# A relative-position bias for attention: one mirrored row in DRAM, read as 128 overlapping rows

## The chip, the cores and the metric

The kernel runs on one core of a Trainium2 chip, in one launch. The metric is the time of one execution on the device in microseconds (us), as a median over runs. Five engines work side by side, each through its own instructions in order: TensorE (PE in the profile; its weight loads are PEld), VectorE (DVE), ScalarE (ACT), GpSimd (POOL) and SyncE (SP), which here only issues transfers. A transfer (DMA) that SyncE issues is carried out by 16 DMA engines; the issuing queue itself goes on, unless the next entry has to wait for something.

## The reference, cut to what matters

The network is two transformer blocks over 512 tokens of width 1024, all in float32. The first block adds three branches: a gated spatial mixer, a pooling branch and a differential attention with 4 heads of two 64-wide score maps each. The attention adds a bias that depends only on the distance between query and key, looked up in 32 buckets per head:

```python
def block(args):
    qi, i = args
    qpos = i * Q_BLOCK + jnp.arange(Q_BLOCK)          # Q_BLOCK = 128
    rel = qpos[:, None] - kpos[None, :]
    bias = rel_bias[t5_causal_bucket(rel)].astype(jnp.float32)
    s = jnp.einsum('bqhcd,bkhcd->bhcqk', qi, k).astype(jnp.float32) * scale
    s = s + bias.transpose(2, 0, 1)[None, :, None]
    s = jnp.where((rel >= 0)[None, None, None], s, -1e30)
    p = jax.nn.softmax(s, axis=-1)
    a = p[:, :, 0] - lam * p[:, :, 1]
    return jnp.einsum('bhqk,bkhd->bqhd', a.astype(v.dtype), v)
```

Since the bias depends on `qpos - kpos` alone, one row of values per head, shifted by one place for each query, holds all of it. Behind the attention come gates, a projection, a gated convolutional feed-forward layer, and a second block with a dilated-window attention and another feed-forward layer, which the change does not touch.

## The kernel before

**Units.** The work is a list of weight units. One unit is one [128, 1024] float32 tile of weights: SyncE loads it (`load`, L165) into one of four buffers `wr`, ScalarE rounds it to its leading part `wh` (L171), VectorE computes the remainder `wl` (L103, called from L178), and TensorE multiplies it in 24 matmuls (three products: leading by leading, leading by remainder, remainder by leading), which take about 5.5 us. The loop at the end of `build` (L1316 to L1336) writes the order out by hand: at each step the matmuls of unit `u`, the rounding of unit `u + 3`, the remainder of `u + 2`, the loads up to unit `u + 6`, then what is done with finished products (`post`), then the fillers that the schedule hangs on that unit (`at(unit, function)`, L1176 to L1242). Every engine and queue works in the order in which this loop emits.

**The order around the change.** The units are `uv0` to `uv3`, `v0` to `v3`, then `q0 k0 q1 k1 b0 b1 q2 k2 q3 k3`, then the gates. `bias_prep` hangs on `v2`. The post of each key unit, `double` (L415 to L425), has ScalarE write a leading part `dbh` (L419) and VectorE a remainder `dbl` (L421), and has SyncE copy each half of both to the other 64 partitions (L424). The first scores, `da_scores(0, 0)`, hang on `k1`; block i of head h comes at unit `k1 + 4h + i`.

**The bias.** `bias_load` fetches a one-hot table `oh` of 33 by 640 and the bucket values `rb`. `bias_prep` multiplies them on TensorE (L504, L505), so that each of four partitions gets the 640 bias values of one head, ordered by position, the last 128 being a large constant that masks the future. VectorE negates them into `bs` (L508, L509). SyncE then writes the four rows to a DRAM tile `bd`, each of them 128 times, one behind the other with a pitch of 641 (L511), and reads each head's area back with a pitch of 640 (L515): row p of the tile `strip[h]` starts one value earlier in the bias row than row p - 1. In `da_scores` the reduction on VectorE (L548) adds a window of the strip to the scores in PSUM and takes the row minimum. It does so twice for each of 4 blocks of 4 heads, 32 times in all, with widths of 128, 256, 384 and 512. ScalarE then takes the exponential, and later units transpose the result and multiply it by the values.

Of the kernel before, what the change touches and what calls it, by code (L numbers as in the profile page):

```python
# [23 lines left out]
F32 = mybir.dt.float32  # L24
# [7 lines left out]
S = 512  # L32
# [23 lines left out]
def build(tc, a):  # L56
    nc = tc.nc
    te, ve, ac, po = nc.tensor, nc.vector, nc.scalar, nc.gpsimd
    ctx = ExitStack()
    with ctx:  # L60
# [58 lines left out]
        def split2(src, name, n=S):  # L119
            """As split; the remainder comes one step later."""  # L120
            hi = slot(name + "h", F32R)
            lo = slot(name + "l", F32R)
            ac.activation(hi[:, :n], src, AF.Copy)
            later(1, tt, lo[:, :n], src, f(hi)[:, :n], OP.subtract)
            return hi, lo

# [1 line left out]
        prm = cp.tile([128, NPRM], F32, name="prm")  # L128
# [14 lines left out]

# [1 line left out]
        units = []  # L145
# [76 lines left out]

# [1 line left out]
        def compact(hl, out, bank=misc):  # L224
            """Sums over the partitions of a [128, 512] tile: [128, 4], token = 128 * column + partition."""
            hi, lo = hl
            p = bank("cs")
            mm(p, onesr, hi, True, False)
            mm(p, onesr, lo, False, True)
            for b in range(4):  # L230
                t = tiny("dg", 128)
                ve.tensor_tensor_reduce(out=t, in0=p[:, 128 * b:128 * b + 128], in1=identf, scale=1.0,
                                        scalar=0.0, op0=OP.mult, op1=OP.add, accum_out=out[:, b:b + 1])
# [4 lines left out]
        def bcast_rows(cols, name):  # L238
            """cols: [128, 4] per-token values -> [128, 512] with them along the free axis."""
            p = misc(name + "p")  # L240
            for b in range(4):
                te.transpose(p[:, 128 * b:128 * b + 128], cols[:, b:b + 1].to_broadcast([128, 128]),
                             identf)
            return p
# [5 lines left out]

        # state shared by the stages
        X, XH, XL = {}, {}, {}
# [17 lines left out]
        def norm_in(m, src, g, key):  # L270
            """hi/lo of src * g, and the square of src."""
            XH[m] = slot("xh", F32R)
            XL[m] = slot("xl", F32R)
            ac.activation(XH[m], src, AF.Copy, scale=g)
            stt(XL[m], src, g, f(XH[m]), OP.mult, OP.subtract)
# [15 lines left out]

        # =================================================================
        # Block 1
        # =================================================================
        UV, GM = {}, {}
# [85 lines left out]

# [1 line left out]
        VH = {}  # L383
# [15 lines left out]
        def stack(src, gain):  # L399
            """Two heads of 64 features: per head the leading part above the remainder (swapped for  # L400
            the second), so that one product over 128 rows takes both."""
            t = duo("stk")
            for e, r, o in halves():
                if gain is None:
                    ac.activation(t[r, e, :], src[r], AF.Copy)
                else:
                    ac.activation(t[r, e, :], src[r], AF.Copy, scale=gain[r])
            for e, r, o in halves():
                if gain is None:
                    tt(t[o, e, :], src[r], f(t)[r, e, :], OP.subtract)  # L410
                else:
                    stt(t[o, e, :], src[r], gain[r], f(t)[r, e, :], OP.mult, OP.subtract)
            return t

        def double(src):  # L415
            """Two heads of 64 features: per head the leading part, and the remainder, in both halves."""
            h, l = duo("dbh"), duo("dbl")
            for e, r, o in halves():
                ac.activation(h[r, e, :], src[r], AF.Copy)  # L419
            for e, r, o in halves():  # L420
                tt(l[r, e, :], src[r], f(h)[r, e, :], OP.subtract)  # L421
            for t in (h, l):
                for e, r, o in halves():
                    nc.sync.dma_start(f(t)[o, e, :], f(t)[r, e, :])  # L424
            return h, l  # L425
# [10 lines left out]

# [1 line left out]
        ZB, YB, pw = {}, {}, {}  # L438
# [49 lines left out]

# [1 line left out]
        strip = {}  # L490
# [10 lines left out]
        def bias_prep():  # L501
# [7 lines left out]
            ve.tensor_scalar(bs[:4, 512:640], p1[:4, :128], -1.0, None, op0=OP.mult)  # L509
            d = dr.tile([4, 128 * 641], F32, name="bd")  # L510
            nc.sync.dma_start(d.rearrange("h (p u) -> h p u", u=641)[:, :, :640],  # L511
                                bs[:4, None, :640].to_broadcast([4, 128, 640]))
            for h in range(4):
                strip[h] = slot("strip")
                nc.sync.dma_start(strip[h], d[h, :128 * 640].rearrange("(p u) -> p u", u=640)[:, 127:639])  # L515

# [15 lines left out]
        def da_scores(h, i):  # L532
# [11 lines left out]
            for c, p in enumerate(pp):  # L544
                if c == 0 or i > 1:
                    ts_ = slot("st")
                t = ts_[:, 256 * c:] if i < 2 else ts_
                ve.tensor_tensor_reduce(out=t[:, :W], in0=p[:, :W], in1=strip[h][:, 384 - 128 * i:],  # L548
                                        scale=1.0, scalar=BIG, op0=OP.add, op1=OP.min,
                                        accum_out=nm[:, c:c + 1])  # L550
                ts.append(t)
# [63 lines left out]

# [1 line left out]
        G, MG = {}, {}  # L617
# [24 lines left out]

# [1 line left out]
        def xhl():  # L644
# [69 lines left out]

# [1 line left out]
        GL, AH, AL = {}, {}, {}  # L716
# [68 lines left out]

        # =================================================================
        # Block 2
        # =================================================================
        st2 = cp.tile([128, 40], F32, name="st2")
# [5 lines left out]
        def b2_stat():  # L795
            """rsqrt of the final norm and of block 2's norm; their product in both token orders."""
            rf, ma, mb, r2 = st2[:, 8:12], st2[:, 12:16], st2[:, 16:20], st2[:, 20:24]
# [42 lines left out]
        def qk_norm(key, scale):  # L840
            """Token-major q/k features [128, 8 x 64] per block -> rms-normalised."""
            def post(p):
# [32 lines left out]
        def qk_tr(key, part, dst, dkey, gain):  # L875
            """Transpose 128 features (2 heads) of all blocks; gain per feature; hi/lo."""
            qs = QK[key]
# [29 lines left out]

        # natural-order part: group 0; statistics per (block, head)
        nst = cp.tile([128, 4, 2, 8], F32, name="nst")
# [26 lines left out]
        def n_tr(pr, j):  # L936
            """Key block j: the queries of blocks j and j+1, per head: [k, (e, q)]."""
            p = misc("ntr")
# [31 lines left out]
        def n_stats(pp):  # L970
            """Statistics of heads 4*pp..4*pp+3 to C order."""
            h = slice(4 * pp, 4 * pp + 4)
# [9 lines left out]
        def c_scores(pr, b0, nb):  # L982
            """Joint softmax of groups 1 and 2 with group 0's statistics, for blocks b = t % 4."""
            w = tp.tile([128, 5, 8], F32, name="cw", tag="cw", bufs=4)
# [61 lines left out]
        def c_tr(pr, b):  # L1046
            """[k, (g, e, q)]"""
            p = misc("ctr")
# [9 lines left out]
        def c_f(pr):  # L1058
            """Group 0's part times its share of the joint softmax."""
            fp = misc("fbp")  # L1060
# [110 lines left out]

        # =================================================================
        # Fillers
        # =================================================================
        L = label
# [67 lines left out]

        # =================================================================
        # Emission
        names.update({v: k for k, v in label.items()})
        # =================================================================
        warm = misc("warm")
# [106 lines left out]
def _layout(inp):  # L1355
# [80 lines left out]
    oh[32, 512:] = 1.0  # L1436
    A["oh"] = oh
    return A
# [16 lines left out]
```

## Time and profile before

| | |
|---|---|
| time, median of 3 runs | 1414.61 us (1413.69 to 1415.21) |
| span of the profiled execution | 1413.5 us; the page gives no other time of it |
| TensorE busy | 1366.0 us, 97% of the span |
| VectorE, ScalarE, GpSimd busy | 57%, 43%, 18% |
| mean granted clock of TensorE | 0.987 |
| the 32 bias reductions (L548) | 284 to 692 ns each, from 116.8 to 217.1 us |
| the write of `bd` (L511) | 1280 KB, issued at 49.6 us |
| the four reads of the strips (L515) | 256 KB each, issued from 102.6 to 103.9 us |

Times in the trace count from the start of the span. A busy matmul's end is modelled, since matmuls are pipelined, so rows of matmuls overlap a little. A row of waits names the waiting operation, its line, and what released it. In the chain of work that ended last, each piece begins where the piece that released it ends.

### The profile page before, as it was taken

To read this page: it belongs to the slowest core of one execution; us is meant where nothing else is said; L and a number is where in the kernel's file an instruction comes from. 1 tells how busy PE (TensorE), PEld (TensorE's weight loads), DVE (VectorE), ACT (ScalarE), POOL (GpSimd) and SP (SyncE) were. 2 spreads that over 40 slices of the span, in tenths; PEclk is the share of its full clock that TensorE was granted. 3 is DMA by queue.
4 is the path that set the end of the run, shared out by engine and by line. 5 is a ranking of instruction groups with operands and counts; after the bars stand their busy time and mean duration, and the time that the engine had idled before them with its cause. 6 is when DMAs were issued, how large, how long until landed. Compare 5 with 4: busy or idle time off the path is not lost.

```text
span 1413.5 us, 16670 instructions
## 1 busy us (share of the span) xinstructions
PE 1366.0 (97%) x6360; PEld 1138.0 (81%) x6360; DVE 808.8 (57%) x1328; ACT 603.3 (43%) x974; POOL 248.9 (18%) x208
## 2 busy tenths in 40 slices
PE   9927999999999999999999999999999999999998
PEld 7816888888888888888888888888878888888887
DVE  6705766555656554553335847567887666665222
ACT  6404654423434333333224657655754444443110
POOL 3204111110111111110113611223061111110000
PEclk9968999999999999999999999999999999999999
DMA  7225422233233323232332333222223333333330
GB/s 251 55 43 159 120 75 89 75 129 125 89 95 100 104 90 105 90 97 82 112 97 75 120 91 90 61 77 73 75 66 99 99 95 98 96 98 93 113 113 32
DMA packets 46692, 135.92 MB, mean 96 GB/s; under 512 B 9923, under 2 KB 10638, under 8 KB 46612
## 3 DMA queue, kind: packets, MB, share of 16 engines
q1 hardware_dynamic: 45556, 132.60, 31.0%
q0 software_dynamic: 912, 2.19, 0.5%
q8 instruction: 50, 0.82, 0.2%
q14 instruction: 30, 0.25, 0.1%
q10 hardware_dynamic: 144, 0.07, 0.0%
HBM read 127.19 MB, written 3.44 MB: 92 GB/s over the span
## 4 chain that ended last, share of the span: by engine, by line
PE 92%; another core or an unknown queue 4%; DVE 2%; DMA 2%; SPq 1%; issue 0%; ACT 0%; DVEq 0%
PE acc L89 84%; PE cs L89 1%; DMA wr<-in_w_uv 1%; PE cu L89 1%; PE qkt L880 1%; PE sc L89 1%; PE nu L89 1%; DVE xl L106 1%; DMA dbl<-dbl 1%; PE ns L89 1%; PE pv L89 1%; PE ctr L1051 0%; PE ms L89 0%; PE ntr L944 0%
## 5 line engine op out<-in xcount | busy, mean ns | idle before, releaser
L89 PE MATMUL acc<-xh,wh 128*128 128x512 f32 x968 | 378.8, 391 | 0.0
L89 PE MATMUL acc<-xl,wh 128*128 128x512 f32 x968 | 377.4, 390 | 0.0
L89 PE MATMUL acc<-xh,wl 128*128 128x512 f32 x968 | 377.3, 390 | 0.0
L103 DVE TENSOR_TENSOR wl<-wr,wh 128x1024 fp32r<-128x1024 f32 (+2 forms) x233 | 297.4, 1277 | 128.6 <-PE acc L89 77.3
L171 ACT ACTIVATE wh<-wr 128x1024 fp32r<-128x1024 f32 (+1 forms) x233 | 242.0, 1039 | 256.6 <-PE acc L89 170.8
L89 PEld LDWEIGHTS acc<-xh,wl 128*128 128x128 f32 x968 | 182.1, 188 | 38.2
L89 PEld LDWEIGHTS acc<-xh,wh 128*128 128x128 f32 x968 | 182.2, 188 | 37.4
L89 PEld LDWEIGHTS acc<-xl,wh 128*128 128x128 f32 x968 | 182.2, 188 | 37.3
L89 PE MATMUL acc<-al,wh 128*128 128x512 f32 (+1 forms) x358 | 138.0, 385 | 0.0
L89 PE MATMUL acc<-ah,wl 128*128 128x512 f32 (+1 forms) x358 | 138.0, 385 | 0.0
L89 PE MATMUL acc<-ah,wh 128*128 128x512 f32 (+1 forms) x358 | 138.0, 385 | 0.0
L720 ACT ACTIVATE cv<-z,prm 128x512 f32<-128x512 f32 x66 | 53.7, 816 | 165.7 <-DVE z L103 165.7
L106 DVE SCALAR_TENSOR_TENSOR cv<-z,prm,cv 128x511 f32<-128x511 f32 (+1 forms) x132 | 99.6, 756 | 2.4
L89 PEld LDWEIGHTS acc<-ah,wh 128*128 128x128 f32 x358 | 67.2, 188 | 13.6
L89 PEld LDWEIGHTS acc<-al,wh 128*128 128x128 f32 x358 | 67.2, 188 | 13.5
L89 PEld LDWEIGHTS acc<-ah,wl 128*128 128x128 f32 x358 | 67.2, 188 | 13.4
L89 PE MATMUL acc<-wh,ch 128*128 128x512 f32 x192 | 75.8, 395 | 0.0
L89 PE MATMUL acc<-wl,ch 128*128 128x512 f32 x192 | 74.9, 390 | 0.0
L89 PE MATMUL acc<-wh,cl 128*128 128x512 f32 x192 | 74.8, 390 | 0.0
L103 POOL TENSOR_TENSOR gl<-cv,r2b 128x512 f32<-128x512 f32 x22 | 28.4, 1291 | 202.9 <-ACT cv L734 202.9
L103 POOL TENSOR_TENSOR act<-cv,cv 128x512 f32<-128x512 f32 x22 | 28.4, 1292 | 202.0 <-DVE cv L106 188.4
L236 POOL TENSOR_TENSOR rr<-ss,mh 128x8 f32<-128x8 f32 x24 | 38.8, 1645 | 114.1 <-DVE ss L852 114.1
(333 smaller groups left out, 1958.1 us busy)
## 6 DMA issues: line engine op xcount, KB each, us to landing
wr<-in_w_up SPq DMA_DIRECT2D x88, 512.0 KB, 3.5
wr<-in_w_dn SPq DMA_DIRECT2D x32, 512.0 KB, 3.5
wr<-in_w_g SPq DMA_DIRECT2D x24, 512.0 KB, 3.5
wr<-in_w_qkc SPq DMA_DIRECT2D x16, 512.0 KB, 3.5
wr<-in_w_o SPq DMA_DIRECT2D x12, 512.0 KB, 3.6
wr<-in_w_dn SPq DMA_DIRECT2D x16, 384.0 KB, 3.1
wr<-in_w_qkn SPq DMA_DIRECT2D x8, 512.0 KB, 4.2
wr<-in_w_vc SPq DMA_DIRECT2D x8, 512.0 KB, 3.4
```

Of the source, the lines that this page charges most:

```text
L89: te.matmul(out, l, r, start=start, stop=stop, skip_group_check=True)
L103: (eng or ve).tensor_tensor(out, x, y, op=op)
L106: ve.scalar_tensor_tensor(out, x, s, y, op0=o0, op1=o1)
L171: ac.activation(hi[:, :n], raws[j][:, :n], AF.Copy)
L236: po.tensor_tensor(out, src, mh[:, :n], op=OP.pow)
L720: ac.activation(c, z, AF.Identity, scale=P(cw, 2 * n + j), bias=P(cb, j))
L880: te.transpose(p[:, 128 * b:128 * b + 128], qs[b][:, 128 * part:128 * part + 128], identf)
```

## The change

The bias row of each head is written to DRAM once, as one row of 640, and the one-hot table is built in reverse order on the host, so the row is mirrored. The strip's row p is read from position p + 1 of that row, 512 values on: 128 overlapping rows with a step of one value. The mirrored strip therefore has to be read from right to left, which a hand-made access pattern with a step of -1 (`mirrored`) does in the bias reduction. Block i uses the first 128 (i + 1) values of the strip, where it used the last ones before. The diff also takes out comments and docstrings, which are not shown.

```diff
@@ bias_prep
-            d = dr.tile([4, 128 * 641], F32, name="bd")
-            nc.sync.dma_start(d.rearrange("h (p u) -> h p u", u=641)[:, :, :640],
-                                bs[:4, None, :640].to_broadcast([4, 128, 640]))
+            d = dr.tile([4, 640], F32, name="bd")
+            nc.sync.dma_start(d, bs[:4, :640])
             for h in range(4):
                 strip[h] = slot("strip")
-                nc.sync.dma_start(strip[h], d[h, :128 * 640].rearrange("(p u) -> p u", u=640)[:, 127:639])
+                row = d[h:h + 1, :]
+                nc.sync.dma_start(strip[h], bass.AP(row.tensor, row.offset + 1, [[1, 128], [1, S]]))
+
+        def mirrored(t, n):
+
+            x = t[:, n - 1:n]
+            return bass.AP(x.tensor, x.offset, [list(x.ap[0]), [-1, n]])
@@ da_scores
-                ve.tensor_tensor_reduce(out=t[:, :W], in0=p[:, :W], in1=strip[h][:, 384 - 128 * i:],
+                ve.tensor_tensor_reduce(out=t[:, :W], in0=p[:, :W], in1=mirrored(strip[h], W),
                                         scale=1.0, scalar=BIG, op0=OP.add, op1=OP.min,
                                         accum_out=nm[:, c:c + 1])
@@ _layout
-    A["oh"] = oh
+    A["oh"] = np.ascontiguousarray(oh[:, ::-1])
```

## The prediction

> **What bounds the kernel now.** I read the page's busy shares first, then the waits of the matmul engine, the chain of work that ended last around the largest of them, the stretches on both sides of it, and the SyncE queue that the chain runs through.
>
> The page: TensorE works 97% of the span, so only a hole in its work, or a lower clock, can be won back. The figures of the DMA issues are KB and median us from issue to landing.
>
> ```profile
> span 1413.5 us, 16670 instructions
> PE 1366.0 (97%) x6360; PEld 1138.0 (81%) x6360; DVE 808.8 (57%) x1328; ACT 603.3 (43%) x974; POOL 248.9 (18%) x208
> dbh<-dbh SPq DMA_DIRECT2D x16, 128.0 KB, 2.3
> bd<-bs SPq DMA_DIRECT2D x1, 1280.0 KB
> wr<-in_w_b SPq DMA_DIRECT2D x2, 512.0 KB, 4.5
> strip<-bd SPq DMA_DIRECT2D x4, 256.0 KB, 3.4
> out_dram<-out SPq DMA_DIRECT2D x7, 256.0 KB, 2.0
> lnrow<-in_lnrow POOLq DMA_DIRECT2D x1, 256.0 KB, 10.4
> ws<-in_wsT POOLq DMA_DIRECT2D x1, 256.0 KB, 11.2
> dst__90<-nst SPq DMA_DIRECT2D x4, 8.0 KB, 3.7
> d<-st SPq DMA_DIRECT2D x1, 2.0 KB, 8.8
> ```
>
> The waits (total us, times, longest). TensorE's largest is one wait of 35.9 us for the duplicated key tile `dbh`; ScalarE lost 42.2 us to a weight load, and SyncE's queue 52.1 us to the write of `bd`.
>
> ```profile
> PE sc L89 <- DMA dbh<-dbh: 35.9, 1, 35.9
> PE sc L89 <- DMA dbl<-dbl: 0.8, 1, 0.8
> ACT wh L171 <- DMA wr<-in_w_b: 42.2, 1, 42.2
> SPq L515 <- DMA bd<-bs: 52.1, 1, 52.1
> ```
>
> The chain (start, length, what) shows these as one event. The 52.14 us piece has no record of its own: it is the write issued at 49.61 under way. Behind it in the queue stand the strip reads, weight loads, and only then the `dbh` and `dbl` copies (L424) that the first scores need.
>
> ```profile
> 49.61 0.82 SPq L511
> 50.44 52.14 another core or an unknown queue
> 102.97 0.43 SPq L515
> ...
> 105.83 0.66 SPq L424
> 106.58 0.54 SPq L424
> 107.21 8.61 DMA dbl<-dbl
> 115.86 0.93 PE sc L89 x3
> 116.80 7.06 PE acc L89 x24
> 123.86 0.47 PE sc L89 x4
> ...
> 142.33 0.40 PE sc L89 x4
> 142.73 5.50 PE acc L89 x24
> 148.23 0.47 PE sc L89 x4
> ```
>
> The stretches (length, then busy us and count of PE, PEld, DVE, ACT, POOL, granted clock, DMA share, GB/s): full before, empty for 35.9 us, then 9.1 us at a mean clock of 0.70, then full again.
>
> ```profile
> 47.60:78.70 31.10, 31.07 (x145) 25.07 (x144) 17.83 (x41) 9.95 (x19) 0.25 (x1) 1.00 0.25 40
> 78.70:114.60 35.90, 0.02 (x1) 0.06 (x1) 3.20 (x4) 3.26 (x4) 0.00 (x0) 0.55 0.45 108
> 114.60:123.70 9.10, 8.26 (x29) 6.72 (x30) 4.22 (x9) 4.17 (x9) 0.00 (x0) 0.70 0.70 218
> 123.70:220.00 96.30, 96.30 (x460) 80.70 (x459) 70.62 (x169) 55.32 (x118) 23.84 (x25) 1.00 0.29 88
> ```
>
> The write moves 1280 KB in 52.14 us, 25 GB/s, in 4 x 128 rows of 2560 B, with the DMA engines 25% busy in the stretch that holds its start. A quarter of 16 is four engines, so 128 rows each and 52.14 / 128 = 0.407 us a row.
>
> **The change part by part.** *The write.* 512 rows become 4, and 1280 KB become 10 KB. It is still issued once, after the same two VectorE copies. At the rate just found, one row for each of four engines costs 0.4 us beside the landing. The trace shows no 10 KB write of this shape; the bounds are 2.0 us (`out`, 256 KB) and 8.8 us (`d<-st`, 2 KB in single words). I take the nearest row in size and direction, 3.7 us (`dst__90<-nst`, 8 KB): landing at 49.61 + 3.7 = 53.3, with 51.6 and 58.4 as ends.
>
> *The reads.* Still four of 256 KB and 128 rows of 2048 B, with a row step of 4 B instead of 2560 B, all out of 2560 B of DRAM. The rows that decide whether this crawls:
>
> ```profile
> 102.59 1.76 SPq L515 DMA_DIRECT2D strip<-bd  x4
> 104.46 0.37 SPq L165 DMA_DIRECT2D wr<-in_w_b  x1
> 66.22 1.28 ACT L419 ACTIVATE dbh<-kt 64x512 fp32r<-64x512 f32 x2 [3.07 <-DVE kt L103]
> 77.64 1.03 PE L376 MATMUL gtr<-identf,gy 128*128 128x128 f32 x8
> L548 DVE CUSTOM_DVE_ANT_0 st<-sc,strip 128x512 f32<-128x512 f32 x8 | 5.2, 688 | 0.2
> L548 DVE CUSTOM_DVE_ANT_0 st<-sc,strip 128x128 f32<-128x128 f32 x8 | 2.0, 288 | 2.1 <-PE sc L89 2.1
> L103 DVE TENSOR_TENSOR gz<-acc,r1b 128x512 f32<-128x512 f32 x8 | 5.5, 690 | 12.3 <-PE acc L89 12.3
> ```
>
> `lnrow` reads one 2 KB row 128 times and landed in 10.4 us, no slower than `ws`, with 128 different rows, in 11.2 us in the same crowded start. So I take 3.4 us, the price of the old strip reads. Ends: 2.0 us (nothing lands sooner here), and one read at 25 GB/s, 10.4 us.
>
> *What stood behind them on SyncE.* The four issues take 1.76 us: 53.3 to 55.1 (60.2 at worst), all landed by about 59. The load of `w_b` follows 0.1 us later, takes 0.37 us to issue and 4.5 us to land: about 60.1, at worst 65.2. Its first reader, ScalarE, is at the key cast of row L419 until 66.22 + 1.28 = 67.5 anyway. So 42.2 us of ScalarE's wait go with 7.4 us in hand (2.3 at worst). Two more weight loads follow; they wait only for their buffers, as in every unit. The `dbh` copies can then go when the cast is done, 67.5, and land 2.3 us later, near 70. `dbl` stands two issues behind (0.66 + 0.54), at 68.7; even at the 8.61 us that it took in the crowd of the chain above it lands by 77.3. TensorE comes to the first scores at 77.64 + 1.03 = 78.7, so 1.4 us are in hand at the worst. VectorE wants the first strip about 81, after the next key's remainders, 22 us after landing.
>
> *TensorE.* From 78.68 it runs what it now runs from 78.68 + 35.9 = 114.58 to 123.86: the four score matmuls of block 0 and one weight unit. The same pair undisturbed stands at 142.33: 0.40 + 5.50 = 5.90 us. So this piece ends at 84.58 instead of 123.86: **39.28 us less**. Of these, 35.9 + 0.8 are the waits; the other 2.5 are matmuls at the low clock after the hole (the unit took 7.06 instead of 5.50; the scores, from 114.58 to 116.80, took 2.22 with the 0.84 of wait, instead of 0.40). These go too, because the clock was 1.00 in the stretches on both sides of the hole.
>
> *The mirrored operand.* 32 score reductions read the strip with step -1. Forward, the widths 512 and 128 take 688 and 288 ns: 400 ns for 384 columns, 1.04 ns each, over 8 x (128 + 256 + 384 + 512) = 10,240 columns 10.7 us in all. No instruction of this trace reads backwards. The lower end is no change: a gain is excluded, since a different two-input operation of 512 columns takes the same 690 ns (`gz`), so the columns, not the order, set the price. The upper end is open; at twice the price it is 10.7 us of VectorE. I take no change, since addresses a word apart are just as near in either direction. Cover: from 123.7 to 220 VectorE is busy 70.62 of 96.3 us, so 25.7 us are free and the twofold price is hidden. Without that cover the cost would be the whole 10.7 us.
>
> [...]
>
> *The rest* (the one-hot table built backwards on the host, comments taken out, a smaller DRAM tile) adds no instruction: nothing.
>
> *Sum.* 1413.5 - 39.3 = 1374.2 us of span. The page gives no time of the profiled execution beside its span; the runs' median, 1414.61, stands 1.1 above it, so I forecast 1414.61 - 39.28 = **1375.3 us**. Late next would be nothing in this place: what follows it in the trace of before, from 123.7 to 220, has TensorE busy for 96.30 of 96.30 us, and its feeders work in step with it. Own range 1373.3 to 1378: 2 below for the spread of the runs (1413.69 to 1415.21), 2.7 above for a short wait that the hole covered.
>
> **The rivals.**
>
> *Something else is late near 79 (part of the gain).* The engines behind TensorE would go without the pause. For it: ScalarE and VectorE queues are in order, and the transposes' evacuation and the first reductions fall together. Against: they stood still in the hole too (3.3 and 3.2 us of work in 35.9), so they gained no lead from it. Price: a wait of 3 to 10 us, and with a long one a low clock after it as now (2.5): 1378 to 1388.
>
> *The overlapping reads crawl.* The write was slow; if the cause was that 512 packets went through one small place and not that four engines did the work, the reads will do the same. For: 25 GB/s. Against: `lnrow`. The price at 25 GB/s: 4 x 256 KB = 1.05 MB in 41.7 us, from 53.4 to 95.1; then the copies land 2.3 to 8.6 us later, 97.4 to 103.7, instead of at 115.86: a gain of 12 to 18, **1396 to 1403**.
>
> [...]
>
> *The write is not what is slow (the change doesn't do what it says).* If the 52 us were a fixed delay of a DRAM write by SyncE before its readers may go, the four rows would wait as long. Against: the `dst` write and its like land in 3.7 us, and the DMA bytes flow evenly at 25 GB/s. The time would be 1414.6.
>
> *Slower: the mirrored read makes VectorE the bound.* With r times the price a column, VectorE gets (r - 1) x 10.7 us more and has 25.7 us to spare: it decides from r = 3.4, and undoes the gain at (r - 1) x 10.7 = 25.7 + 39.3, r = 7.1. At r = 8 the time is 1375.3 + 74.9 - 25.7 = **1424**. For it: nothing in the trace reads backwards. Against: a step back of one word would have to cost seven steps forward, and no row here hints at a price for the order.
>
> **How the numbers follow.** The forecast 0.85; a smaller late wait 0.06; the crawl 0.05; no effect 0.01; slower 0.03. The range must leave out no more than 0.2. The forecast with its own range leaves out 0.15 and what falls beyond its ends; I take 1373.3 to 1380, which reaches into the small-wait case and leaves out the crawl and the slow mirror. A change within 0.2% is 2.8 us, about what this measurement can tell from none. Faster: 0.85 + 0.06 + 0.05 = 0.96. Same 0.01. Slower 0.03.
>
> **What the changed profile would show.** The wait of SyncE's queue at the strip reads falls from 52.1 us to 2 to 9 us; the strip issues stand near 53, not 102.59; the 35.9 us wait for `dbh` is gone from TensorE's list and the chain has no unknown piece; the granted clock stays 1.00 through 47 to 220 us; the strip reads land in about 3.4 us; the L548 groups keep 688 and 288 ns. The prediction is wrong if the strips land over 10 us, if the first scores wait for a copy, or if L548 takes more than three times as long.

## The result, and the profile after

| | before | changed |
|---|---|---|
| time, median | 1414.28 us (1413.69 to 1415.21, 4 runs) | 1375.25 us (1374.88 to 1375.68, 4 runs) |
| ratio | | 0.9721, 95% interval 0.9707 to 0.9735 |
| span of the profiled execution | 1413.5 us | 1373.8 us |

The forecast was 1375.3 us. The page and the transfer list of the changed kernel: the span is 39.7 us shorter at nearly the same TensorE work (1363.8 against 1366.0 us), so a hole was closed.

```profile
span 1373.8 us, 16670 instructions
PE 1363.8 (99%) x6360; PEld 1137.4 (83%) x6360; DVE 808.5 (59%) x1328; ACT 603.2 (44%) x974; POOL 248.7 (18%) x208
strip<-bd SPq DMA_DIRECT2D x4, 256.0 KB, 4.0
bd<-bs SPq DMA_DIRECT2D x1, 10.0 KB
```

What SyncE's queue waited for between 47 and 80 us, and what it issued. The wait for the write fell from 52.1 to 1.1 us. The strip reads follow the write by 1.50 us from issue to issue, not 52.98, and the key copies go as soon as their data are cast, at 66.39.

```profile
SPq L165 <- DVE wl L103: 17.2, 4, 6.5
SPq L424 <- ACT dbh L419: 4.5, 2, 2.4
...
SPq L515 <- DMA bd<-bs: 1.1, 1, 1.1
```

```profile
49.12 0.33 SPq L511 DMA_DIRECT2D bd<-bs  x1
50.62 1.77 SPq L515 DMA_DIRECT2D strip<-bd  x4
52.49 0.38 SPq L165 DMA_DIRECT2D wr<-in_w_b  x1
...
66.39 1.18 SPq L424 DMA_DIRECT2D dbh<-dbh  x2
67.66 1.19 SPq L424 DMA_DIRECT2D dbl<-dbl  x2
```

The chain at the same place and the stretches: the transposes (`gtr`), the first scores and the unit behind them stand end to end, 0.40 + 5.51 us, and the clock is 1.00 from 47 to 220 us.

```profile
77.31 0.87 PE gtr L376 x8
78.18 0.40 PE sc L89 x4
78.58 5.51 PE acc L89 x24
84.09 0.47 PE sc L89 x4
```

```profile
78.70:84.60 5.90, 5.90 (x29) 4.98 (x28) 4.70 (x10) 4.20 (x10) 0.00 (x0) 1.00 0.71 191
47.00:220.00 173.00, 173.00 (x824) 144.14 (x823) 121.25 (x274) 90.62 (x179) 33.76 (x32) 1.00 0.34 101
```

The unit behind the first scores ends at 84.09 instead of 123.86: 39.77 us, of which 0.49 is an earlier arrival (the bias product started at 47.23 instead of 47.72). The difference, 39.28, is the prediction's sum. That it agrees to the last digit is partly luck: between the medians the gain is 39.03 us, and between the spans 39.7. The backward reductions, now L553, cost what the forward ones did:

```profile
L553 DVE CUSTOM_DVE_ANT_0 st<-sc,strip 128x512 f32<-128x512 f32 x8 | 5.2, 687 | 0.2
...
L553 DVE CUSTOM_DVE_ANT_0 st<-sc,strip 128x128 f32<-128x128 f32 x8 | 2.0, 287 | 2.0 <-PE sc L89 1.9
```

### The profile page after: what moved, and what is told of

It reads as the page before. It is cut to its first block, busy times and chain, and to the rows that moved or that the text cites. A ratio compares the mean times of both kernels' runs of the same rounds, so it can differ in the third digit from the quotient of the medians.

```text
span 1373.8 us, 16670 instructions
## 1 busy us (share of the span) xinstructions
PE 1363.8 (99%) x6360; PEld 1137.4 (83%) x6360; DVE 808.5 (59%) x1328; ACT 603.2 (44%) x974; POOL 248.7 (18%) x208
## 4 chain that ended last, share of the span: by engine, by line
PE 98%; DVE 1%; issue 0%; ACT 0%; DMA 0%; DVEq 0%; POOLq 0%
PE acc L89 89%; PE ms L89 2%; PE cs L89 1%; PE cu L89 1%; PE qkt L885 1%; PE nu L89 1%; PE sc L89 1%; PE ns L89 1%; PE pv L89 1%; DVE xl L106 1%; PE ctr L1056 0%; PE ntr L949 0%; PE tr L583 0%; DVE y L103 0%; DMA g<-in_prm 0%
```

## The experiments

The theory: the write of 512 rows by four DMA engines held SyncE's queue, and all that stood behind it came late; overlapping reads and the backward operand (the strip read from right to left) cost nothing. Rivals: the reads or the backward operand have prices of their own; many packets from one small place are slow whatever the engines; the bias data themselves were late, not the queue.

**How much of the write hurts: 128, 64 and 32 copies.** The changed kernel with the write blown up again; only the first copy is read.

```diff
-            d = dr.tile([4, 640], F32, name="bd")
-            nc.sync.dma_start(d, bs[:4, :640])
+            d = dr.tile([4, 128, 640], F32, name="bd")      # or 64, or 32
+            nc.sync.dma_start(d, bs[:4, None, :640].to_broadcast([4, 128, 640]))
...
-                row = d[h:h + 1, :]
+                row = d[h, 0:1, :]
```

> The changed kernel, but the four rows are written 128 times again (unused beyond the first); mirrored row, overlapping reads and backward reduction stay. If the write alone made the hole, the strip reads are issued 53 us after the write again and the time is that of before, 1414.3 us within 1.5. If the overlapping reads or the backward operand gave or cost anything of their own, it lies off 1414.3 by that amount.

> The changed kernel with 64 copies. From the two traces the strip reads follow the write by 52.98 us for 128 copies and 1.50 for one, 0.405 us a copy; 64 copies give 27.0 us, strip reads at 76.1. Before, the first scores could run 12.0 to 13.3 us after the first strip read was issued: 88 to 89.4 here, against 78.2 undisturbed. So a hole of about 11 us and some 2 us of low clock: 1388 us (1385 to 1391). If every microsecond of the write cost one, it would be 1375.3 + 25.5 = 1400.8.

> The changed kernel with 32 copies: strip reads at 63.2, everything behind them landed by 76.4, before TensorE needs it at 78.2. If the slack of the prediction is real, 12.6 us more of write cost nothing: 1375.3 us within 1.5. If every microsecond of the write cost one: 1387.8.

Measured, against 1415.11 us of the kernel before on the same chip: 128 copies 1417.7 us (ratio 1.0017, 1.0007 to 1.0027), 64 copies 1393.09 (0.9844, 0.9829 to 0.9859), 32 copies 1378.17 (0.9736, 0.9722 to 0.9751). From the write's issue to the strip reads it took 52.98, 27.38 and 14.57 us, so 0.400 us for each copy from 32 on. The rows for 64 copies:

```profile
49.15 0.83 SPq L511 DMA_DIRECT2D bd<-bs  x1
76.53 1.76 SPq L515 DMA_DIRECT2D strip<-bd  x4
78.39 0.37 SPq L165 DMA_DIRECT2D wr<-in_w_b  x1
81.58 1.54 SPq L424 DMA_DIRECT2D dbh<-dbh  x2
83.22 1.34 SPq L424 DMA_DIRECT2D dbl<-dbl  x2
```

The shape is the theory's, a slack and then a slope: 32 copies cost about 3 us, the next 32 cost 15, the next 64 cost 25, which is 0.38 us a copy. But each time lies above what was expected, by 3 to 5 us; 0.8 us of this is the level of the series, whose kernel before took 1415.11 and not 1414.28. The transfer rows show one more cause: in these three kernels the strips landed in 5.9, 5.6 and 5.4 us, against 3.4 before, and the transfers behind them were held up. The rows above have the key copies issued 5.05 us after the strip reads (76.53 to 81.58); in the kernel before it was 3.24 us. The 32-copy kernel's list of TensorE's waits has `dbl` at 0.9 us, where the expectation had it land in time. Its bias product also started at 49.04, 1.8 us later than in the changed kernel's trace; the start of the program moves by that much between traces. Of the 3.2 us by which its span is longer (1377.0 against 1373.8), 1.8 thus stand ahead of the write and 0.9 are the wait, so 3 us probably overstates what 32 copies cost.

**What makes the reads slow.** 128 copies, mirrored row and backward reduction as above, but row p of a strip comes from copy p.

```diff
-                nc.sync.dma_start(strip[h], bass.AP(row.tensor, row.offset + 1, [[1, 128], [1, S]]))
+                nc.sync.dma_start(strip[h], bass.AP(row.tensor, row.offset + 1, [[641, 128], [1, S]]))
```

> The kernel with 128 copies and the mirrored row again, but row p of a strip is read from copy p (row step 641 values) instead of all from the first copy; the backward reduction stays. With all rows from one copy the strips landed in 5.9 us at 143 to 225 GB/s, against 3.4 us at 330 to 430 GB/s in the kernel before, and the time was 0.17% above that of before. If many rows from one place are what is slow, the strips land in about 3.4 us again, the wait for dbh is about 36 us and not 39, and the time is that of before. If the backward operand cost those 2.6 us, the time stays 0.17% above and the landing at about 3.4 or 5.9 either way.

Measured: 1414.47 us against 1415.42 before, 0.9994 (0.9985 to 1.0004). TensorE's long wait was 37.1 us, between the 36 that was expected and the 39.0 of overlapping rows. The strips land as before the change; first this kernel's row, then that of the kernel with 128 copies whose rows overlap:

```profile
strip<-bd SPq DMA_DIRECT2D x4, 256.0 KB, 3.5
```

```profile
strip<-bd SPq DMA_DIRECT2D x4, 256.0 KB, 5.9
```

So 128 overlapping rows out of one 2560 B row are slower by 2.4 us at the median, and in the kernel whose queue is late that shows as 0.17% of the time. The backward reduction stays in both, and the kernel with a copy for each row takes the time of the old one: reading backwards costs nothing that can be measured. In the changed kernel the slow reads are hidden, since its strips land (4.0 us, from 50.62 on) long before the first reduction at 80.17.

**The engines or the place.** The kernel before, but its 128 copies are made by a second transfer, DRAM to DRAM, with 128 as the outermost dimension.

```diff
+            d0 = dr.tile([4, 640], F32, name="bd0")
+            nc.sync.dma_start(d0, bs[:4, :640])
+            d = dr.tile([128, 4, 640], F32, name="bd")
+            nc.sync.dma_start(d, d0[None, :, :].to_broadcast([128, 4, 640]))
...
+                row = d[0:1, h, :]
+                nc.sync.dma_start(strip[h], bass.AP(row.tensor, row.offset + 127, [[2559, 128], [1, S]]))
```

> The kernel before (128 copies, skewed forward reads), but the 128 copies are made by a second transfer from DRAM to DRAM whose outermost dimension is 128, so that it can use 16 engines. By the theory that four engines at 0.405 us a row made the write slow, 32 rows an engine take 13 us: strip reads at about 65, first scores at 77 to 79, 1375 to 1378 us. By the rival that many packets through one small place are slow, it takes 52 us again and the time is 1414 to 1417.

Measured: 1376.36 us (0.9724, 0.9709 to 0.9738). SyncE's queue:

```profile
51.39 0.33 SPq L511 DMA_DIRECT2D bd<-bs  x1
53.00 0.58 SPq L513 DMA_DIRECT2D bd<-bd  x1
60.59 1.77 SPq L517 DMA_DIRECT2D strip<-bd  x4
```

The packets tell more. These rows are the kernel before while it wrote (49.7 to 102.5 us) and this kernel during its second transfer (53 to 60.5 us):

```profile
DMA packets 519, 1.34 MB, mean 25 GB/s; under 512 B 5, under 2 KB 5, under 8 KB 517
DMA packets 144, 1.31 MB, mean 175 GB/s; under 512 B 16, under 2 KB 16, under 8 KB 16
```

The same 1280 KB were written within 7.6 us instead of 52. So the mirrored row and the overlapping reads are one way to the gain, not the only one, and reading the same 10 KB of DRAM 128 times is not what takes 52 us.

What made the old write slow is not settled by this, because three things changed together. The old write went in 512 packets of 2560 B, never more than four at once; the new one in 128 packets of 10 KB, up to about 16 at once; and the new one starts from DRAM, not from four partitions of `bs`. At most four packets at once went with an outermost dimension of 4, up to about 16 with one of 128; no run shows this apart from the other two changes. That the number of engines set the rate is not borne out by the packet records of the traces. In the old write a packet takes 0.373 us, and four are started in every 0.400 us: 4 x 2560 B in 0.400 us, 25.6 GB/s. In the changed kernel the four packets go one after the other, 0.100 us each: 2560 B in 0.100 us, again 25.6 GB/s. Four at once moved no more than one at a time, which speaks for a limit that the four shared. Whether that is the four source partitions, and whether more engines would have helped there, no run shows. The same rows written from many partitions, or copied from DRAM with 4 outermost, would tell.

**The queue or the data.** The kernel before, with write and strip reads issued by GpSimd.

```diff
-            nc.sync.dma_start(d.rearrange("h (p u) -> h p u", u=641)[:, :, :640],
+            nc.gpsimd.dma_start(d.rearrange("h (p u) -> h p u", u=641)[:, :, :640],
...
-                nc.sync.dma_start(strip[h], d[h, :128 * 640].rearrange("(p u) -> p u", u=640)[:, 127:639])
+                nc.gpsimd.dma_start(strip[h], d[h, :128 * 640].rearrange("(p u) -> p u", u=640)[:, 127:639])
```

> The kernel before with its slow write and the four strip reads issued by GpSimd instead of SyncE. Nothing stands behind them on SyncE any more, so keys and weights arrive; but the strips still land at about 107. By the theory the queue set the hole to 115.9: now the first reduction on VectorE waits from about 80 to 107, the remainder of the weights for unit q2 waits behind it, TensorE stops at about 90 and goes on at about 110: 20 us and 2.5 of low clock, 1398 us (1393 to 1403). If the bias data themselves set the hole, nothing is won: 1415. If the write by this queue spreads over more engines, 1375 to 1380.

Measured: 1404.39 us (0.9929, 0.9915 to 0.9944), above the expected span of 1393 to 1403, and by another way. Its waits on TensorE, and its transfers issued from 48 to 104 us (median us to landing):

```profile
PE sc L89 <- DMA dbh<-dbh: 15.0, 1, 15.0
PE sc L89 <- DMA dbl<-dbl: 11.1, 2, 8.8
```

```profile
bd<-bs POOLq DMA_DIRECT2D x1, 1280.0 KB, 55.8
wr<-in_w_q SPq DMA_DIRECT2D x2, 512.0 KB, 25.4
wr<-in_w_k SPq DMA_DIRECT2D x2, 512.0 KB, 24.7
wr<-in_w_b SPq DMA_DIRECT2D x1, 512.0 KB, 4.2
dbh<-dbh SPq DMA_DIRECT2D x4, 128.0 KB, 24.1
```

SyncE's queue did not wait for the write, and yet TensorE stopped at the first scores again: the key copies and weight loads that were issued during the write took 22 to 25 us to land (medians), where 2.3 and 4.5 stand in the list of the kernel before. The queue was slow too: a pair of key copies, issued in 1.2 us in the changed kernel, took 5.7 to 7.9 us to issue. So the write delays others also without standing ahead of them in their queue. The rival that the bias data themselves set the hole is out: TensorE went on at 104.0 us, and the first strip was used only at 109.9. The 20 us that VectorE's late strips should have cost did not come on top: VectorE did wait 27.8 us for a strip, in the shadow of the other wait.

The packets say where the delay came from. GpSimd's write, too, went about four packets at once: from 48 to 104 us its queue's packets took 21.1% of the time of 16 engines, 3.4 of them in the mean. Each of the two loads issued at 55.44 and 62.32 has 128 packets of 4 KB; 96 of each moved within 4 us of the issue, and a quarter of each not before 71 us. That fits four of 16 engines busy with the write, each load having a quarter of its packets on them; which engine moved a packet is not in the records.

**How much more VectorE could have borne.** The prediction hid a doubled price of the backward operand under VectorE's free time. Three versions repeat reductions: all of them twice, all four times, or only blocks 2 and 3 twice; the last ran beside the changed kernel itself.

```diff
-                ve.tensor_tensor_reduce(out=t[:, :W], in0=p[:, :W], in1=mirrored(strip[h], W),
+                for _ in range(2):          # or 4; or 2 if i > 1 else 1
+                    ve.tensor_tensor_reduce(out=t[:, :W], in0=p[:, :W], in1=mirrored(strip[h], W),
```

> The changed kernel with each of the 32 backward reductions done twice: 32 x (486 + 84) ns = 18 us more of VectorE, more than a doubled price of the backward operand would be. VectorE is free for 25.5 of the 95.4 us from 84.6 to 180, so by the prediction's cover it is hidden: 1375.3 us, at most 3 more. If VectorE's order matters at once, up to 1393.

> The changed kernel with each backward reduction done four times: 55 us more of VectorE against 25.5 us free. By the prediction's working TensorE waits for the rest: 1375.3 + 29 = 1404 us (1398 to 1412). If more of VectorE's work can slide past 180, less: 1385 to 1398.

> The changed kernel with only the reductions of blocks 2 and 3 (widths 384 and 512) done twice: 8 x (552 + 84) + 8 x (688 + 84) ns = 11.3 us more of VectorE, close to the 10.7 us that a doubled price of the backward operand would be. Doubling all of them cost 6.5 us, with one wait of 3.4 us and a low clock after it, although 18 us fitted into the 25.5 free ones. If the prediction's cover holds for a doubled price, the time is that of the changed kernel within 1.5 us. If the free time is in the wrong places, a wait of 1 to 3 us and a low clock: 2 to 5 us above.

> The changed kernel itself, as the measure for the run beside it: 1375 us within 1.5.

Measured: all twice 1381.73 us, all four times 1403.36, the wide ones twice 1378.66, the changed kernel 1376.10. All twice was expected at 1375.3, at most 3 more, and missed. The wide ones came out by the second branch of their expectation, a wait and 2 to 5 us more, not by the prediction's cover. Both show that the cover leaks: 11.3 us more of VectorE cost 2.6 us although, by the sum, twice that was free, and 18 us cost about 6. Four times came out close to the expected 1404, but in part by luck: TensorE's waits from 47 to 260 us add up to 18.2 us, not 29; the rest lies at least in part in a lower clock, 0.91 from 124 to 220 us. TensorE's wait with the wide ones twice, and two stretches of that kernel:

```profile
PE sc L89 <- DVE nm L554: 2.1, 1, 2.1
```

```profile
90.00:112.00 22.00, 22.00 (x103) 18.32 (x102) 17.88 (x39) 8.46 (x18) 14.52 (x16) 1.00 0.27 75
112.00:130.00 18.00, 15.90 (x66) 12.78 (x65) 14.73 (x38) 11.19 (x25) 0.00 (x0) 0.91 0.36 115
```

Over these stretches VectorE is not full, 17.88 of 22 and 14.73 of 18 us. But its chain around the wait goes back and forth with ScalarE. First the two operations of VectorE that had to wait between 112 and 122 us, then the chain:

```profile
113.77 1.39 DVE L103 TENSOR_TENSOR stk<-qt,stk 64x512 fp32r<-64x512 f32 x2 [1.54 <-ACT stk L405]
120.06 1.41 DVE L103 TENSOR_TENSOR dbl<-kt,dbh 64x512 fp32r<-64x512 f32 x2 [1.43 <-ACT dbh L419]
```

```profile
113.77 0.69 DVE stk L103
114.47 0.69 DVE stk L103
115.95 1.14 DVE wl L103
117.08 0.66 DVE A L106
118.82 0.68 ACT st L561 x3
119.50 0.53 ACT dbh L419
120.06 0.69 DVE dbl L103
120.77 0.69 DVE dbl L103
121.49 0.56 DVE st L554
122.71 0.73 PE sc L89 x2
```

Each exponential needs a reduction and each remainder a cast, and both engines work in order. VectorE stands still 1.54 and 1.43 us until a cast is done and is nearly full in between, from 114 to 118 us and from 120 us on. Such idle moments belong to the chain and can't be filled at will.

## Why the prediction was right, point by point

- *The hole and its cause.* Right. The wait of 35.9 us, the one of 0.8 and 2.5 us of low clock are gone, and nothing took their place. Blowing the write up again brings the old time back (ratio 1.0017 with overlapping reads, 0.9994 without). This is the step that the forecast rests on.
- *Four engines as the reason for the slow write.* Not shown, and doubtful. At most four packets ran at once, as the share of 0.25 said, but together they moved 25.6 GB/s, no more than one packet at a time in the changed kernel. The prediction read how many were at work as what bounded them. The sum did not suffer: the rate that it took, 0.4 us for four rows, holds either way, and in the changed kernel the four packets took 0.38 us.
- *The write's landing.* Taken as 3.7 us within 2.0 and 8.8; the strip reads were issued 1.50 us after the write, so it was below the lower bound. The bounds came from transfers of other shapes, and that nothing lands sooner than 2.0 us, as the prediction says of the reads, was a misreading: the same list has an output of 128 KB at 1.7. It cost nothing, because every deadline behind it had several us in hand.
- *The reads at 3.4 us.* Mis-sized: 4.0 us here, and 5.4 to 5.9 with other loads behind them. The row that spoke against a crawl, `lnrow`, was itself in a crowd, where it took 10.4 us, and so could not show a difference of two. The rival of the crawl was right in kind and far off in size: 2.4 us, not 38.
- *Nothing late next.* Right: TensorE's list of waits has no entry from 47 to 260 us.
- *The mirrored operand at no change.* Right to 1 ns (687 and 287 against 688 and 288). The kernel from which the 0.17% vanished reads backwards too.
- *The cover for a doubled price.* Wrong, though the price never came: 11.3 us of added work cost 2.6. The step that failed is the one that compared a sum of work with a sum of free time over 96 us. Had reading backwards cost twice as much, the forecast would have been too low by about that.

## What to carry to other kernels

A transfer whose wait blocks a queue is worth its wait only from the point where something behind it misses its deadline: list what stands behind it and when each is first used, and the gain can be worked out, here 39.3 us against 39.0 measured. Look at the DMA share while a slow transfer runs: here 0.23 from 49.7 to 102.5 us, at 25 GB/s, went with at most four packets under way, and did not show that more engines would help. Compare with the rate of one packet alone; here it was the same 25.6 GB/s. Free time of an engine covers added work only where its chain with the other engines has room; a stretch average doesn't show that: here 11.3 us more, against 25.5 free, cost 2.6.

## What was not expected of the hardware

A slow write issued from another queue still held up others: loads and copies issued by SyncE beside it landed in 22 to 25 us instead of 2.3 to 4.5, with a quarter of a load's packets held back. Four packets of 2560 B at once, read from four partitions of SBUF, moved 25.6 GB/s together, as much as one at a time. And 128 rows of 2 KB that all lie within one 2560 B row were read more slowly than 128 rows from 128 places, 5.9 against 3.5 us for a strip of 256 KB with the same loads queued behind.
